# A hybrid attention/recurrence layer on one core: a front projection threaded through the transposes, and the sixth token block's closing products on GpSimd

## The chip, the core and the metric

One core of one Trainium2 chip runs the whole layer in one launch. The engines are TensorE (PE, with its weight loads PEld), VectorE (DVE), ScalarE (ACT), GpSimd (POOL) and SyncE (SP), which issues most DMAs. The metric is the device time of one execution in microseconds (us), as a median over several runs.

## The reference

The layer takes `x` of 1024 tokens by 1024 channels. It normalises the tokens, projects them with one wide matrix, runs two attention-like branches on the result, merges them, adds the residual, and ends in a squared-ReLU MLP and a last RMS norm. Cut to what the change touches:

```python
xn = rmsnorm(x, norm1_g[layer])
u = xn @ w_in[layer]                       # q, k, v of the attention come first
q_sb, k_sb, v_sb, ... = jnp.split(u, ...)
...
hn = rmsnorm(h, norm2_g[layer])
a = jnp.square(jax.nn.relu(hn @ w_ff1[layer]))
h = h + a @ w_ff2[layer]
return rmsnorm(h, final_g)
```

`rmsnorm(t, g)` is `t * rsqrt(mean(t*t) + 1e-6) * g` for each token.

## The kernel before

Everything is kept in float32 precision by splitting each operand of a matmul into a rounded part ("hi") and a remainder ("lo" = value minus hi). A product is then three matmuls: hi by hi, lo by hi, hi by lo. `hi_copy` (L156, on ACT) makes a hi part, `lo_sub` (L161, on DVE) makes a remainder. TensorE works through one long list of such triples, and the other engines prepare its operands and take its results out of the eight PSUM banks.

The tokens lie in eight blocks of 128 (`x` tile number `tb`). **The front** (the last part of the file, from `first_norms` on) does this for blocks 0 and 1, then for 2 and 3, then for 4 to 7: sum of squares on ACT and DVE, root on GpSimd (`inv_root`, L274), scaling on DVE (L664), and `norm_transpose`, in which TensorE turns the scaled tokens channel group by channel group (`kt` 0 to 7, tiles `xnt`, L131), ACT writes the hi part `xnh` with the gain (L348), and DVE the remainder `xnl` (L351). A bank of `xnt` is free again when its `xnl` is made. With one bank for the first projection and two for the values, five are left for `xnt`.

Between these steps `st.advance(n, 1)` takes n steps of the first job (`first_job`): the projection of the first head's queries and keys (`pjqk`, weights `wqk0`) and the projection to values (`pjv`, weights `wv`). The value weights come in four pieces of 1024 columns, each for two `kt`: raw `wvr`, hi `wvh`, remainder `wvl`. The body's steps are: four of `pjqk` for blocks 0 and 1, four "quarters" of `pjv` for blocks 0 and 1 (hi products of `kt` 0, 1; of `kt` 2, 3; remainder products of `kt` 0, 1; of `kt` 2, 3), four of `pjqk` for blocks 2 and 3, then the rest of `pjv`.

What sets the order: each engine runs its instructions in the order of its own list. That list follows the order in which the code is written, refined by a scheduler that honours priorities; `in_turn` and `after` add edges that fix the order on ACT and DVE while `turns["on"]` is true. A remainder that is "owed" (`owed_wlo`) is emitted later, by `lo_now()`; piece 1 of `wv` is such a one.

**The end** is `mlp_down`, whose last step treats the four column blocks of the last product m6 one after another. When block `tb` of four is done, DVE adds it to the residual tile `hb` of token block 2*tb+1 (`land`), ACT sums the squares of the right half (`half_ssq`), GpSimd adds that to the left half's (L2147) and takes the root (L274), and `finish_tokens` (L2156) makes the output. For an odd block the left half was multiplied with the gain earlier, so ACT only scales it (L2163); the right half takes `hb * root * gain` on DVE (L2166). The sixth token block (number 5, `NT - 3`) is finished while the last block (number 7) is summed, its right half after `summed_up`. The last block is done in quarters of 256 columns.

Of the kernel before, what the change touches and what calls it, by code (L numbers as in the profile page):

```python
# [9 lines left out]
F32 = mybir.dt.float32  # L10
# [4 lines left out]
ALU = mybir.AluOpType  # L15
# [7 lines left out]
NT = T // P  # L23
# [16 lines left out]
def kernel(  # L40
# [100 lines left out]
    def lo_now(behind=None):  # L141
        while owed_wlo:
            after(owed_wlo.pop()(), behind)
# [128 lines left out]
    def inv_root(mean, name):  # L272
        y = small.tile([P, 1], F32, tag="rs_y1", name=f"{name}_y", bufs=4)
        nc.gpsimd.tensor_tensor(out=y, in0=mean, in1=expo[:, 0:1], op=ALU.pow)  # L274
        return y
# [12 lines left out]
    last_power = [None]  # L288
# [33 lines left out]
    def norm_transpose(acts, half, b0, n, between=None):  # L322
# [17 lines left out]
        for kt in range(KT):  # L340
# [18 lines left out]
            )  # L359

# [84 lines left out]
    class Unit:  # L445
# [28 lines left out]
        def split(self, upto=None):  # L474
            self.load(upto)
            self.hl = self.hl or []
            for i, r in list(enumerate(self.raw))[len(self.hl) : upto]:
# [7 lines left out]
                if self.name == "wf1" or self.name == "wv" and i == 1:  # L485
                    hi_copy(h, r)
                    owed_wlo.append(lambda h=h, l=l, r=r: lo_sub(l, r, h))
                    continue
# [235 lines left out]
    def first_job():  # L724
# [17 lines left out]

        def v_steps(tb, kts):
# [1391 lines left out]
    def half_ssq(tb, n):  # L2135
# [10 lines left out]
        else:  # L2146
            nc.gpsimd.tensor_scalar(  # L2147
                out=ssq, in0=ssq, scalar1=1.0 / D, scalar2=fin[tb, 0], op0=ALU.mult, op1=ALU.add
            )

    def finish_tokens(tb, earlier=None, sides=(0, 1)):
        if sides[0] == 0:
            roots[tb] = inv_root(fin[tb, 1], f"fr{tb}"), slot(f"y{tb}")
        r, y = roots[tb]
        parts = 2 if tb == NT - 1 else 1
        for n, cs in (  # L2156
# [5 lines left out]
            if tb % 2 == 1 and n == 0:  # L2162
                after(nc.scalar.mul(y[:, cs], hres[tb][:, cs], r), earlier)  # L2163
# [93 lines left out]
    def mlp_down():  # L2257
        for i, (gi, c) in enumerate(steps):
# [11 lines left out]
            else:  # L2270
                for tb in range(3):
# [10 lines left out]
                for part in (slice(0, 256), slice(256, 512)):  # L2282
# [3 lines left out]
                    if part.start == 0:  # L2286
# [3 lines left out]
                        finish_tokens(NT - 3, squared, (0,))  # L2290
# [3 lines left out]
                summed_up = add(mean, mean, ssq)  # L2294
                finish_tokens(NT - 3, summed_up, (1,))
# [213 lines left out]
```

## Time and profile before

| | us |
|---|---|
| median of 3 runs | 1420.7 (1420.46 to 1420.71) |
| the profiled execution | 1420.47 |
| its span in the profile | 1418.7 |
| TensorE busy in it | 1408.6 (99%) |
| VectorE busy | 1088.1 (77%) |
| ScalarE busy | 684.6 (48%) |
| GpSimd busy | 143.3 (10%) |

The times of the views below are microseconds from the start of the span. A timeline row reads: start, duration, engine, line, operation, output from inputs, shape, how many were merged into the row, and in brackets how long the engine was idle before and what ended that. Several instructions of a row overlap a little, so a row of n with a single one beside it gives the distance between two starts. The span leaves out 1.8 us of the execution's time, before its first and after its last instruction.

### The profile page before, as it was taken

Reading aid. Unit: us, or ns where it says so; the run is one execution under the profiler, and the core shown is the slowest. Engines: PE = TensorE matmul, PEld = TensorE weight load, DVE = VectorE, ACT = ScalarE, POOL = GpSimd, SP = SyncE. Lnnn points to the kernel's source line nnn. Section 1 sums busy time; section 2 is a strip of 40 time slices with the busy share of each in tenths; the row PEclk is TensorE's granted clock in tenths of the full one; section 3 lists DMA queues with packets and bytes.
Section 4 is the critical chain, followed back from the end, with each engine's and each line's share of the span. In section 5 each row is a group of like instructions: output and inputs, shape, how many; then the busy total and the mean of one; then the engine's idle time right before and its main releaser. Section 6 shows DMA issues by size and latency. Waiting matters only on the chain.

```text
span 1418.7 us, 18796 instructions
## 1 busy us (share of the span) xinstructions
PE 1408.6 (99%) x6848; PEld 1184.0 (83%) x6848; DVE 1088.1 (77%) x1494; ACT 684.6 (48%) x1182; POOL 143.3 (10%) x339
## 2 busy tenths in 40 slices
PE   9999999999999999999999999999999999999998
PEld 8888888888888888888888888888888888888886
DVE  7579988988567888887788897677766657768766
ACT  6356676664243554433334764445444443434343
POOL 3012223210011031000000300000000000000031
PEclk9999999999999999999999999999999999999999
DMA  7124445545135685364585514444446974776725
GB/s 238 30 67 127 105 100 98 106 76 155 62 74 167 227 222 182 124 215 156 160 299 193 185 53 170 163 162 139 143 144 239 351 268 152 278 273 240 277 93 187
DMA packets 163173, 237.72 MB, mean 168 GB/s; under 512 B 26332, under 2 KB 93448, under 8 KB 163080
## 3 DMA queue, kind: packets, MB, share of 16 engines
q1 hardware_dynamic: 146056, 190.37, 40.0%
q0 software_dynamic: 11584, 34.61, 10.0%
q10 hardware_dynamic: 5440, 11.54, 2.3%
q8 instruction: 54, 0.88, 0.3%
q14 instruction: 39, 0.32, 0.1%
HBM read 168.32 MB, written 66.06 MB: 165 GB/s over the span
## 4 chain that ended last, share of the span: by engine, by line
PE 98%; DVE 1%; ACT 1%; DMA 0%; issue 0%; POOL 0%; SPq 0%; POOLq 0%; DVEq 0%; ACTq 0%
PE pm L128 21%; PE pX L128 9%; PE pW L128 6%; PE pY L128 6%; PE pjqk L128 6%; PE pga L128 4%; PE gX L128 4%; PE gY L128 4%; PE pjf L128 3%; PE pjq L128 3%; PE pys L128 3%; PE pji L128 3%; PE pyh L128 3%; PE pjv L128 3%; PE po L128 3%; PE z L128 2%
## 5 line engine op out<-in xcount | busy, mean ns | idle before, releaser
L156 ACT CAST whid<-w 128x1024 fp32r<-128x1024 f32 x30 | 31.6, 1054 | 154.4 <-PE pm L128 89.7
L826 DVE TENSOR_TENSOR_SCAN rm<-rm,bits 128x511 f32<-128x511 f32 (+7 forms) x72 | 87.3, 1220 | 17.0 <-ACT rm L804 16.9
L128 PE MATMUL pm<-whid,sh 128*128 128x512 f32 x240 | 93.4, 389 | 0.0
L128 PE MATMUL pm<-wlod,sh 128*128 128x512 f32 x240 | 93.4, 389 | 0.0
L128 PE MATMUL pm<-whid,sl 128*128 128x512 f32 x240 | 93.4, 389 | 0.0
L128 PE MATMUL pm<-tl,sh 128*128 128x512 f32 (+1 forms) x210 | 81.3, 387 | 0.0
L128 PE MATMUL pm<-th,sl 128*128 128x512 f32 (+1 forms) x210 | 81.3, 387 | 0.0
L128 PE MATMUL pm<-th,sh 128*128 128x512 f32 (+1 forms) x210 | 81.3, 387 | 0.0
L161 DVE TENSOR_TENSOR wlod<-w,whid 128x1024 fp32r<-128x1024 f32 x30 | 36.7, 1223 | 54.5 <-ACT whid L156 54.5
L161 DVE TENSOR_TENSOR sl<-sa,sh 128x1024 fp32r<-128x1024 f32 x56 | 68.2, 1218 | 0.3 <-ACT sh L156 0.3
L156 ACT CAST wTh<-pw 128x512 fp32r<-128x512 f32 (+2 forms) x96 | 43.8, 485 | 41.9 <-PE pw L131 41.0
L156 ACT CAST sh<-sa 128x1024 fp32r<-128x1024 f32 x56 | 57.2, 1046 | 7.8 <-DMA sa<-ad 7.8
L2143 POOL TENSOR_SCALAR fss<-fss 128x1 f32<-128x1 f32 x8 | 3.9, 482 | 562.0 <-ACT fsc L2138 561.5
L161 DVE TENSOR_TENSOR wTl<-pw,wTh 128x512 fp32r<-128x512 f32 (+2 forms) x96 | 49.9, 546 | 3.9 <-ACT wTh L156 3.7
L128 PEld LDWEIGHTS pm<-wlod,sh 128*128 128x128 f32 x240 | 45.0, 188 | 9.5
L128 PEld LDWEIGHTS pm<-whid,sl 128*128 128x128 f32 x240 | 45.1, 188 | 9.3
L128 PEld LDWEIGHTS pm<-whid,sh 128*128 128x128 f32 x240 | 45.1, 188 | 9.3
L169 DVE TENSOR_TENSOR bt<-bt,rm 128x511 f32<-128x511 f32 (+7 forms) x72 | 48.9, 685 | 3.5
L804 ACT ACTIVATE rm<-z 128x511 f32<-128x511 f32 (+4 forms) x96 | 48.0, 500 | 5.5 <-PE z L128 2.9
L128 PE MATMUL pX<-sqh,t1l 128*128 128x512 f32 x128 | 49.9, 390 | 0.0
L128 PE MATMUL pX<-sql,t1h 128*128 128x512 f32 x128 | 49.9, 390 | 0.0
L128 PE MATMUL pX<-sqh,t1h 128*128 128x512 f32 x128 | 49.8, 389 | 0.0
(930 smaller groups left out, 4432.4 us busy)
## 6 DMA issues: line engine op xcount, KB each, us to landing
w<-in_w_ff_dram SPq DMA_DIRECT2D x72, 512.0 KB, 4.7
sa<-ad SPq DMA_DIRECT2D x52, 512.0 KB, 6.4
ad<-a SPq DMA_DIRECT2D x32, 256.0 KB, 4.5
ad<-s SPq DMA_DIRECT2D x16, 512.0 KB, 3.3
tw<-in_w_out_dram POOLq DMA_DIRECT2D x24, 256.0 KB, 4.5
pr<-pd SPq DMA_DIRECT2D x10, 512.0 KB, 6.0
x<-in_x_dram SPq DMA_DIRECT2D x8, 512.0 KB, 7.8
xnl<-xnh POOLq DMA_DIRECT2D x8, 512.0 KB, 6.4
```

The lines of the kernel that those rows point to most:

```text
L128: return pe(nc.tensor.matmul(*a, **k))
L156: hi_last[0] = after(in_turn("act", nc.scalar.copy(dst, src)), hi_behind[0])
L161: nc.vector.tensor_tensor(out=dst, in0=src, in1=hi.bitcast(F32), op=ALU.subtract),
L169: return nc.vector.tensor_tensor(out=out, in0=a, in1=b, op=ALU.mult)
L804: nc.scalar.activation(rm[:, s0 + c0 - 1 : s0 + m - 1], z[:, c0:m], AF.Sigmoid, scale=-0.125)
L826: sc = nc.vector.tensor_tensor_scan(out=rr, data0=rr, data1=bits[:, 1024 - nk + a : 1024 - nk + b][:, ::-1], initial=rm[:, b : b + 1] if i ...
L2143: nc.gpsimd.tensor_scalar(out=ssq, in0=ssq, scalar1=1.0 / D, scalar2=EPS, op0=ALU.mult, op1=ALU.add)
```

## The change

Four edits in the front:

- `u_v.split()` now stands ahead of `norm_transpose(xn, 0, 2, 2)` instead of behind it, so the hi parts of the pieces 2 and 3 of `wv` are cast by ACT before the hi parts `xnh` of blocks 2 and 3.
- The remainder of piece 2 is made on GpSimd (L493). The remainders of the pieces 1 and 3 are both owed, and `lo_now()` stands behind `norm_transpose`; it pays them in the order in which they were owed.
- The last quarter of `pjv` (remainder products of `kt` 2, 3) moves behind the four `pjqk` steps of blocks 2 and 3.
- `norm_transpose` gets a callback `then`, called behind each `kt`; for blocks 2 and 3 it takes one `pjqk` step behind `kt` 4, 6 and 7. The number of steps taken up to the norms of blocks 4 to 7 is the same.

And two at the end:

- For block 5, GpSimd multiplies `hb` with the gain for the right half, in two quarters of 256 columns (`times_gain`, L2168): the first one once block 5's tile has landed, the second behind block 5's root.
- `finish_tokens(NT - 3)` then takes both halves on ACT behind the squares of the last block's first quarter: the right half is scaled from the product `y` instead of being made by DVE.

```diff
     def lo_now(behind=None):
         while owed_wlo:
-            after(owed_wlo.pop()(), behind)
+            after(owed_wlo.pop(0)(), behind)
...
-    def norm_transpose(acts, half, b0, n, between=None):
+    def norm_transpose(acts, half, b0, n, between=None, then=None):
...
+            if then:
+                then(kt)
...
-                if self.name == "wf1" or self.name == "wv" and i == 1:
+                if self.name == "wf1" or self.name == "wv" and i in (1, 3):
                     hi_copy(h, r)
                     owed_wlo.append(lambda h=h, l=l, r=r: lo_sub(l, r, h))
+                    continue
+                if self.name == "wv" and i == 2:
+                    hi_copy(h, r)
+                    ins = nc.gpsimd.tensor_tensor(
+                        out=l, in0=r, in1=h.bitcast(F32), op=ALU.subtract
+                    )
+                    after(ins, turns["dve"])
                     continue
...
         def body():
             ps = bank(f"{name}_0")
             yield from qk_steps(ps, 0, 0, 2)
-            for hi in (True, False):
-                for k0 in (0, 2):
-                    for tb in range(2):
-                        for kt in (k0, k0 + 1):
-                            v_part(tb, kt, hi, not hi)
-                    yield
+            for hi, k0 in ((True, 0), (True, 2), (False, 0)):
+                v_quarter(hi, k0)
+                yield
             yield from qk_steps(ps, 0, 2, 2)
+            v_quarter(False, 2)
+            yield
             ep(ps, 0)
...
+    def times_gain(tb, c0, behind):
+        cs = slice(c0, c0 + 256)
+        return after(
+            nc.gpsimd.tensor_tensor(
+                out=roots[tb][1][:, cs], in0=hres[tb][:, cs], in1=gfb[0][:, cs], op=ALU.mult
+            ),
+            behind,
+        )
...
-            if tb % 2 == 1 and n == 0:
-                after(nc.scalar.mul(y[:, cs], hres[tb][:, cs], r), earlier)
+            if tb % 2 == 1 and n == 0 or tb == NT - 3:
+                after(nc.scalar.mul(y[:, cs], (hres[tb], y)[n][:, cs], r), earlier)
...
                     landed = land(6, tb)
-                    half_ssq(2 * tb + 1, 1)
+                    if tb == 2:
+                        y = slot(f"y{NT - 3}")
+                        roots[NT - 3] = None, y
+                        product = times_gain(NT - 3, 512, None)
+                    half_ssq(2 * tb + 1, 1, product if tb == 2 else None)
                     if tb:
                         finish_tokens(2 * tb - 1, landed)
+                roots[NT - 3] = inv_root(fin[NT - 3, 1], f"fr{NT - 3}"), y
+                times_gain(NT - 3, 768, last_root[0])
...
-                        finish_tokens(NT - 3, squared, (0,))
+                        finish_tokens(NT - 3, squared)
...
-                summed_up = add(mean, mean, ssq)
-                finish_tokens(NT - 3, summed_up, (1,))
+                add(mean, mean, ssq)
                 finish_tokens(NT - 1)
...
     norm1((2, 3), half_means((2, 3)))
+    u_v.split()
+    st.advance(3, 1)
+    norm_transpose(xn, 0, 2, 2, then=lambda kt: st.advance(1, 1) if kt in (4, 6, 7) else None)
     lo_now()
-    st.advance(3, 1)
-    norm_transpose(xn, 0, 2, 2)
-    u_v.split()
-    st.advance(5, 1)
+    st.advance(2, 1)
```

How the lists of the engines move. First TensorE in the front, from the fifth pair of transposes of blocks 2 and 3 on (`x_165` and `x_169` are these blocks, `xnt_2` the banks they are turned into, `wvl_295` the remainder of `wv`'s piece 1). Before:

```order
L131 MATMUL xnt_2_358<-ident,x_169 128x128
L131 MATMUL xnt_2_363<-ident,x_165 128x128
L131 MATMUL xnt_2_363<-ident,x_169 128x128
L131 MATMUL xnt_2_368<-ident,x_165 128x128
L131 MATMUL xnt_2_368<-ident,x_169 128x128
L128 MATMUL pjv_316<-wvl_295,xnh_237 128x512
L131 MATMUL xnt_2_373<-ident,x_165 128x128
L131 MATMUL xnt_2_373<-ident,x_169 128x128
L128 MATMUL pjv_316<-wvl_295,xnh_237 128x512
L128 MATMUL pjv_321<-wvl_295,xnh_237 128x512 x2
L128 MATMUL pjqk_0_265<-xnh_229,wqk0whi 128x256
```

and now, from the same place on:

```order
L131 MATMUL xnt_2_364<-ident,x_169 128x128
L128 MATMUL pjqk_0_265<-xnh_229,wqk0whi 128x256
L128 MATMUL pjqk_0_265<-xnl_230,wqk0whi 128x256
L128 MATMUL pjqk_0_265<-xnh_229,wqk0wlo 128x256
L128 MATMUL pjqk_0_265<-xnh_229,wqk0whi 128x256
L131 MATMUL xnt_2_375<-ident,x_165 128x128
L128 MATMUL pjqk_0_265<-xnl_230,wqk0whi 128x256
L128 MATMUL pjqk_0_265<-xnh_229,wqk0wlo 128x256
L131 MATMUL xnt_2_375<-ident,x_169 128x128
L131 MATMUL xnt_2_380<-ident,x_165 128x128
L131 MATMUL xnt_2_380<-ident,x_169 128x128
```

The next rows of the list are the rest of `pjqk` with the last pair of transposes; it ends so:

```order
L128 MATMUL pjqk_0_265<-xnl_254,wqk0whi 128x256
L128 MATMUL pjqk_0_265<-xnh_253,wqk0wlo 128x256
L128 MATMUL pjqk_0_265<-xnh_253,wqk0whi 128x256
L128 MATMUL pjqk_0_265<-xnl_254,wqk0whi 128x256
L128 MATMUL pjqk_0_265<-xnh_253,wqk0wlo 128x256
L128 MATMUL pjv_322<-wvl_295,xnh_237 128x512 x2
L128 MATMUL pjv_327<-wvl_295,xnh_237 128x512 x2
L128 MATMUL pjv_322<-wvh_315,xnh_245 128x512
```

The four products with the remainder of piece 1 stood between the last transposes, and stand now behind all 24 products of `pjqk`, which are threaded among the last six transposes.

VectorE in the front, from the scaling of block 3 on. Before:

```order
L664 TENSOR_SCALAR x_169<-x_169,n_3_y 128x1024
L161 TENSOR_TENSOR wvl_295<-wvr_167,wvh_294 128x1024
L351 SCALAR_TENSOR_TENSOR xnl_230<-xnt_2_338,prm,xnh_229 128x256
L351 SCALAR_TENSOR_TENSOR xnl_230<-xnt_2_343,prm,xnh_229 128x256
L351 SCALAR_TENSOR_TENSOR xnl_238<-xnt_2_348,prm,xnh_237 128x256
L351 SCALAR_TENSOR_TENSOR xnl_238<-xnt_2_353,prm,xnh_237 128x256
L351 SCALAR_TENSOR_TENSOR xnl_246<-xnt_2_358,prm,xnh_245 128x256
L351 SCALAR_TENSOR_TENSOR xnl_246<-xnt_2_363,prm,xnh_245 128x256
L351 SCALAR_TENSOR_TENSOR xnl_254<-xnt_2_368,prm,xnh_253 128x256
L351 SCALAR_TENSOR_TENSOR xnl_254<-xnt_2_373,prm,xnh_253 128x256
L161 TENSOR_TENSOR wvl_379<-wvr_171,wvh_378 128x1024
L161 TENSOR_TENSOR wvl_383<-wvr_173,wvh_382 128x1024
```

and now:

```order
L673 TENSOR_SCALAR x_169<-x_169,n_3_y 128x1024
L351 SCALAR_TENSOR_TENSOR xnl_230<-xnt_2_344,prm,xnh_229 128x256
L351 SCALAR_TENSOR_TENSOR xnl_230<-xnt_2_349,prm,xnh_229 128x256
L351 SCALAR_TENSOR_TENSOR xnl_238<-xnt_2_354,prm,xnh_237 128x256
L351 SCALAR_TENSOR_TENSOR xnl_238<-xnt_2_359,prm,xnh_237 128x256
L351 SCALAR_TENSOR_TENSOR xnl_246<-xnt_2_364,prm,xnh_245 128x256
L351 SCALAR_TENSOR_TENSOR xnl_246<-xnt_2_375,prm,xnh_245 128x256
L351 SCALAR_TENSOR_TENSOR xnl_254<-xnt_2_380,prm,xnh_253 128x256
L351 SCALAR_TENSOR_TENSOR xnl_254<-xnt_2_391,prm,xnh_253 128x256
L161 TENSOR_TENSOR wvl_295<-wvr_167,wvh_294 128x1024
L161 TENSOR_TENSOR wvl_320<-wvr_173,wvh_319 128x1024
```

The remainder of piece 1 moves from ahead of the eight `xnl` to behind them, and that of piece 2 leaves VectorE.

GpSimd at the end, from block 3's sum on (`fss` are sums of squares, `fr_y` roots, `y_12322` the output tile of block 5). Now:

```order
L2160 TENSOR_SCALAR fss_1_12298<-fss_1_12298,fss_0_12054 128x1
L274 TENSOR_TENSOR fr_y<-fss_1_12298,expo 128x1
L2168 TENSOR_TENSOR y_12322<-hb_10470,gf 128x256
L2160 TENSOR_SCALAR fss_1_12324<-fss_1_12324,fss_0_12114 128x1
L274 TENSOR_TENSOR fr_y<-fss_1_12324,expo 128x1
L2168 TENSOR_TENSOR y_12322<-hb_10470,gf 128x256
L274 TENSOR_TENSOR fr_y<-f_ms,expo 128x1
```

Before, the same list held the two sums and the three roots alone; the two products of 256 columns are new, one ahead of block 5's sum and one between its root and the last block's. VectorE's list at the end is the same but for the product of block 5's right half, which is gone; ScalarE's has one scaling of 512 columns more, and the scaling of block 3's left half now stands behind the squares of block 5 instead of ahead of them. Behind the front and ahead of the end, the lists of all engines read as before.

More of the change, by code (lines that the diff above doesn't have):

```diff
@@ L273, in inv_root @@
         y = small.tile([P, 1], F32, tag="rs_y1", name=f"{name}_y", bufs=4)
-        nc.gpsimd.tensor_tensor(out=y, in0=mean, in1=expo[:, 0:1], op=ALU.pow)
+        last_root[0] = nc.gpsimd.tensor_tensor(out=y, in0=mean, in1=expo[:, 0:1], op=ALU.pow)
         return y
@@ L286, in mean_square @@
         return out
-    last_power = [None]
+    last_power, last_root = [None], [None]
     last_evac = [None]
@@ L741, in v_part, with v_quarter @@
                 matmul(ps, sh, wl, start=False, stop=kt == KT - 1)
+        def v_quarter(hi, k0):
+            for tb in range(2):
+                for kt in (k0, k0 + 1):
+                    v_part(tb, kt, hi, not hi)
         def v_steps(tb, kts):
@@ L2133, with half_ssq @@
     roots = {}
-    def half_ssq(tb, n):
+    def half_ssq(tb, n, behind=None):
         ssq = small.tile([P, 1], F32, tag=f"fss{n}", name=f"fss{tb}_{n}", bufs=8)
@@ L2146, in half_ssq @@
         else:
-            nc.gpsimd.tensor_scalar(
+            ins = nc.gpsimd.tensor_scalar(
                 out=ssq, in0=ssq, scalar1=1.0 / D, scalar2=fin[tb, 0], op0=ALU.mult, op1=ALU.add
             )
+            after(ins, behind)
+    def times_gain(tb, c0, behind):
[6 more added lines that the diff above has]
+        )
     def finish_tokens(tb, earlier=None, sides=(0, 1)):
-        if sides[0] == 0:
+        if tb not in roots:
             roots[tb] = inv_root(fin[tb, 1], f"fr{tb}"), slot(f"y{tb}")
```

## The prediction

> **What bounds the kernel now.** I read the page first, then who waited for whom on TensorE, then the timeline of the two stretches that the change touches.
>
> ```profile
> span 1418.7 us, 18796 instructions
> PE 1408.6 (99%) x6848; PEld 1184.0 (83%) x6848; DVE 1088.1 (77%) x1494; ACT 684.6 (48%) x1182; POOL 143.3 (10%) x339
> PE warm L128 <- POOL ident masks.py:199: 2.2, 1, 2.2
> PE po L128 <- DVE wTl L161: 0.3, 1, 0.3
> PE pjqk L128 <- DVE xnl L351: 0.3, 1, 0.3
> PE xnt L131 <- DVE xnl L351: 0.2, 1, 0.2
> ```
>
> TensorE is busy 99% of the span, and its waits add up to 3.0 us, of which 2.2 are the start. So the time is TensorE's list from end to end, plus what stands around it. A delay of TensorE in the front is paid in full, since there is no later wait that could take it up; other engines' savings count only where TensorE waits for them, or behind its last matmul.
>
> The front, where blocks 2 and 3 are turned:
>
> ```profile
> 16.45 0.39 PE L128 MATMUL pjv<-wvh,xnh 128*128 128x512 f32 x1
> 16.68 0.39 PE L128 MATMUL pjv<-wvh,xnl 128*128 128x512 f32 x1
> 17.82 1.25 PE L131 MATMUL xnt<-ident,x 128*128 128x128 f32 x10
> 18.23 3.03 ACT L348 ACTIVATE xnh<-xnt,prm 128x256 fp32r<-128x256 f32 x8 [3.13 <-PE xnt L131]
> 18.23 0.47 ACT L348 ACTIVATE xnh<-xnt,prm 128x256 fp32r<-128x256 f32 x1 [3.13 <-PE xnt L131]
> 17.60 1.22 DVE L161 TENSOR_TENSOR wvl<-wvr,wvh 128x1024 fp32r<-128x1024 f32 x1
> 18.74 3.23 DVE L351 SCALAR_TENSOR_TENSOR xnl<-xnt,prm,xnh 128x256 fp32r<-128x256 f32 x8
> 18.74 0.48 DVE L351 SCALAR_TENSOR_TENSOR xnl<-xnt,prm,xnh 128x256 fp32r<-128x256 f32 x1
> 19.28 0.83 PE L131 MATMUL xnt<-ident,x 128*128 128x128 f32 x4 [0.21 <-DVE xnl L351]
> 23.85 0.28 PE L128 MATMUL pjqk<-xnh,wqk0wlo 128*128 128x256 f32 x1
> 23.97 0.40 PE L128 MATMUL pjv<-wvh,xnh 128*128 128x512 f32 x1
> ```
>
> Ten transposes fill the five free banks; then TensorE waits until the first `xnl` frees one. It goes on at 19.28, 0.06 us after that `xnl` ends (18.74 + 0.48 = 19.22). From the rows I take the distances between starts: a transpose 0.11 ((1.25 - 0.27) / 9, the last lasting some 0.27), a product of 256 columns 0.12 (23.85 to 23.97), of 512 columns 0.23 (16.45 to 16.68), an `xnl` 0.39 ((3.23 - 0.48) / 7). At 23.97 the first product with pieces 2 and 3 starts. From 17.82 to there the work is 16 transposes (1.74), 24 products of `pjqk` (2.88) and four with piece 1's remainder (0.91): 5.5 of 6.15 us. The waits in it are worth 0.6 us, and that is all that threading could win here.
>
> **The front's cost.** First, what opens the chain does not move. The first `xnh` ends at 18.23 + 0.47 = 18.70, so the first `xnl` can start no earlier than about 18.75 even with VectorE free. Piece 1's remainder ended there anyway: taking it from ahead of the `xnl` wins at most 0.05 us.
>
> Behind them it costs. TensorE resumes at 19.28 and issues, up to the last pair of transposes, eleven products (1.32) and four transposes (0.44): the last pair starts at 21.04 and 21.15 and ends at 21.42, about 1 us later than now. ScalarE's last `xnh` starts at 21.45, where it now starts at 20.75 (18.23 + 3.03 less one of 0.5), ends at 21.95, and the last `xnl` lies at about 22.0 to 22.48 instead of ending at 21.97. Then comes piece 1's remainder with its 1.22, whose start overlaps the end before it by some 0.08: 22.40 to 23.62. TensorE, which has had nothing left since about 22.8, starts the four products with it at 23.68 and the first product of pieces 2 and 3 at 23.68 + 4 x 0.226 = 24.58. That is **0.6 us later** than 23.97. Were the last `xnl` not pushed at all, it would be 21.97 - 0.08 + 1.22 + 0.06 + 0.90 = 24.07, a loss of 0.1; one more slip of an `xnl` (0.39) makes it 1.0. The value is the worked chain, 0.6, and the ends 0.1 and 1.0.
>
> The other moved work has cover, if the loads are there. The casts of pieces 2 and 3 go into ScalarE's idle 3.13 us ahead of `xnh`:
>
> ```profile
> SPq L136 <- DMA wvr<-in_w_in_dram: 3.5, 4, 1.1
> 14.91 0.25 SPq L136 DMA_DIRECT2D prow<-in_lb_logits_dram  x1
> 16.27 0.25 SPq L136 DMA_DIRECT2D prow<-in_lb_logits_dram  x1
> 14.34 0.67 ACT L629 ACTIVATE n1scr<-x 128x512 f32<-128x512 f32 x1
> 21.10 2.05 ACT L156 CAST wvh<-wvr 128x1024 fp32r<-128x1024 f32 x2
> ```
>
> SyncE waits four times for a piece of `wvr`, and its issues at 14.91 and 16.27 follow the third and the fourth: so they land at about 14.87 and 16.23. ScalarE is free at 15.1 and casts them at 15.1 to 16.2 and 16.3 to 17.4, 0.8 us ahead of `xnh`. Without that cover a cast of 1.1 would delay `xnh` by what it overhangs.
>
> GpSimd's remainder of piece 2 waits for the first of these casts and stands behind block 3's root:
>
> ```profile
> 15.13 1.76 POOL L274 TENSOR_TENSOR n_y<-n_ms,expo 128x1 f32<-128x1 f32 x2 [7.39 <-DVE n_ms L1284]
> 16.93 0.75 DVE L664 TENSOR_SCALAR x<-x,n_y 128x1024 f32<-128x1024 f32 x1
> 24.73 0.55 POOL L269 TENSOR_TENSOR n_y<-n_ss,expo 128x1 f32<-128x1 f32 x1
> 25.32 0.75 DVE L664 TENSOR_SCALAR x<-x,n_y 128x1024 f32<-128x1024 f32 x1 [0.72 <-POOL n_y L269]
> 25.37 0.75 POOL L265 TENSOR_SCALAR n_ss<-n_ss 128x1 f32<-128x1 f32 x1
> masks.py:199 POOL TENSOR_SCALAR_AFFINE_SELECT ident<-ident 128x128 f32<-128x128 f32 x1 | 0.3, 287 | 0.0
> L862 POOL MEMSET wTh<- 128x128 f32 x32 | 10.7, 411 | 8.3 <-PE po L128 7.0 <-DVE bt L169 0.7 <-DMA od<-osb 0.5
> 1368.41 0.19 POOL L2143 TENSOR_SCALAR fss<-fss 128x1 f32<-128x1 f32 x1
> 34.88 3.65 PE L131 MATMUL xnt<-ident,x 128*128 128x128 f32 x32
> ```
>
> No row shows GpSimd on a wide product. From 128 columns in 0.287 us I take 2.24 ns a column: 0.57 us for 256 columns, 2.3 for 1024. The low end takes the 0.19 of a one-column sum as a fixed cost: (0.287 - 0.19) / 128 is 0.76 ns a column on top of it, 0.38 and 1.0; the high end is the 0.411 row's 3.2 ns: 0.82 and 3.3. GpSimd is free at 16.89. The rows at 25.3 show what follows: VectorE's scaling starts 0.04 after the root, GpSimd's next 0.05 later still, and that one lasts 0.75 instead of some 0.2 alone; it is held until the scaling is over. So the remainder runs from about 17.7 to 20.0 (21.0 at the high end). TensorE needs it at 25.0, and piece 3's remainder, on VectorE until 24.8, at 26.4: no cost. Roots of blocks 4 to 7 follow on GpSimd, with at most some 0.2 us lost behind VectorE's two remainders, and their tiles are wanted at 34.9. [...]
>
> **The end.** Behind the last matmul stands a chain of small steps:
>
> ```profile
> 1409.09 0.69 DVE L1284 TENSOR_TENSOR hb<-hb,pm 128x512 f32<-128x512 f32 x1 [1.37 <-PE pm L128]
> 1409.70 0.75 DVE L2166 SCALAR_TENSOR_TENSOR y<-hb,fr_y,gf 128x512 f32<-128x512 f32 x1
> 1410.64 0.27 POOL L2147 TENSOR_SCALAR fss<-fss,fss 128x1 f32<-128x1 f32 x1 [1.82 <-ACT fsc L2138]
> 1410.99 0.55 POOL L274 TENSOR_TENSOR fr_y<-fss,expo 128x1 f32<-128x1 f32 x1
> 1412.34 0.48 DVE L281 CUSTOM_DVE_ANT_0 fsc<-hb,fss 128x256 f32<-128x256 f32 x1
> 1413.02 0.74 DVE L2166 SCALAR_TENSOR_TENSOR y<-hb,fr_y,gf 128x512 f32<-128x512 f32 x1
> 1413.18 0.99 POOL L274 TENSOR_TENSOR fr_y<-f_ms,expo 128x1 f32<-128x1 f32 x1 [1.64 <-DVE f_ms L1284]
> 1414.20 0.91 ACT L2163 ACTIVATE y<-hb,fr_y 128x256 f32<-128x256 f32 x2 [1.38 <-POOL fr_y L274]
> ```
>
> The last root takes 0.99 where block 5's takes 0.55, because VectorE's product for block 5 (1413.02) runs beside it. The change takes that product away: **0.44 us won**, if the root starts no later. But the two new products lie ahead of it in GpSimd's list. Block 5's tile lands at 1409.78; by then VectorE's product for block 3 has run since 1409.70, and it holds GpSimd to 1410.45 by the same rule as at 25.3. The first quarter then ends at 1411.07, the sum lies at 1411.15 to 1411.42, the root at 1411.50 to 1412.05, the second quarter at 1412.13 to 1412.70. VectorE wants its squares of the last quarter at 1412.34, in the middle of that. If GpSimd does not hold VectorE, the root starts at 1413.18 as now: -0.44. If the squares wait for the second quarter, they start at about 1412.75, 0.41 later, and nothing is left of the gain: -0.03. With 0.82 a quarter and VectorE held all through it loses 0.47. One row bears on it:
>
> ```profile
> L2166 DVE SCALAR_TENSOR_TENSOR y<-hb,fr_y,gf x13: 476/744/779, 1368.4 to 1414.6; 128x512 f32<-128x512 f32 x11, 128x256 f32<-128x256 f32 x2
> ```
>
> The longest of these products, 779 ns against 744, is the one that starts at 1368.4, with the sum at 1368.41 beside it, which was not held. So VectorE can be the one that gives way. I take 0.0, nearest to the case in which it waits, with -0.44 and +0.47 as ends. ScalarE's extra scaling of block 5 (0.7) ends by 1413.7, ahead of 1414.2; block 3's left half, scaled later, is written out beside the rest. If that cover went, the last scaling would start late by the overhang.
>
> [...]
>
> The sum is +0.6 + 0.0 on the profiled execution's 1420.47, which is 0.2 below the median; on the median of 1420.7 it is **1421.3 us**. By itself it lies between 1420.7 + 0.1 - 0.4 = 1420.4 and 1420.7 + 1.0 + 0.4 = 1422.1.
>
> **The rivals.** *Not slower:* the front loses only its floor of 0.1 and the end keeps its 0.44: 1420.4. For it speaks that short GpSimd quarters would end ahead of 1412.34 (0.38 each gives 1412.32); against it that the last pair of transposes stands behind eleven products. *Slower by more:* at 16.93 GpSimd's wide product takes the turn before block 3's scaling. The scaling, held for 2.3 us, would end at 20.1, TensorE, which turns block 3 from 17.9 on, would stand still for it, and all behind it moves by 2.4: 1421.3 + 2.4 = 1423.7 (1422.4 to 1424.7 by the ends of that price). It decides when GpSimd starts first; the start rows have VectorE ahead by 0.05, and only the row at 1368.41 shows GpSimd unhindered. *No effect:* TensorE's 0.6 us of waits might be refilled just as the threading means, with piece 1's remainder ready in time; VectorE's list, eight `xnl` and then 1.22 us, leaves no room for that, so it gets little.
>
> **How the numbers follow.** The forecast gets 0.64, the not-slower rival 0.2, the scaling held up 0.09, no effect 0.03 (1420.7), anything else 0.04. The predicted time is 1421.3, and the range 1420.2 to 1422.1 leaves out the held scaling and little more. A difference of 0.2%, 2.8 us, is about what a measurement of this kernel can tell from no change: the forecast, the first rival and no effect all lie within it. Slower by more comes from the held scaling where it costs above 2.2 (0.06) and from the rest (0.01), faster by more from the rest alone (0.02).
>
> **What would show it.** In the changed profile TensorE should wait some 0.9 us for `wvl` ahead of the four products of piece 1, the first product of piece 2 should start near 24.6, and the last `xnh` near 21.45. GpSimd's wide remainder should start near 17.7 and last 2.3; block 3's scaling should start at 16.93. At the end the last root should take 0.55, and VectorE's last squares start near 0.4 later behind the matmuls than now. A first product of piece 2 ahead of 24.0 would make the front wrong, squares on time the end; a TensorE wait anywhere between 30 and 1400 us would make the whole sum wrong.

## The result, and the profile after

| | before | after |
|---|---|---|
| median, us | 1420.82 (1420.33 to 1421.09, 22 runs) | 1422.84 (1421.17 to 1424.58, 22 runs) |
| ratio | | 1.0015, 95% interval 1.0009 to 1.0021 |
| the profiled execution, us | 1420.47 | 1421.17 |
| its span, us | 1418.7 | 1419.4 |

The changed kernel is 2.0 us (0.14%) slower, where 0.5 was forecast (1421.3 against this median of 1420.82), and the time lies outside the range. Its executions fall into groups: 19 of 22 lie between 1422.5 and 1423.1, one at 1421.17, two near 1424.5. The profiled execution is the single one at 1421.17. What happens in the rest is seen in a second profile, that of the first experiment, and its rows stand here beside the first's.

The changed kernel's own execution (1421.17), from the head of its page and its waits on TensorE (total, times, longest):

```profile
span 1419.4 us, 18801 instructions
PE 1409.2 (99%) x6848; PEld 1184.0 (83%) x6848; DVE 1086.1 (77%) x1492; ACT 685.3 (48%) x1183; POOL 151.6 (11%) x342
PE warm L128 <- POOL ident masks.py:199: 2.2, 1, 2.2
PE pjv L128 <- DVE wvl L161: 0.6, 1, 0.6
```

and its timeline in the front, engine by engine:

```profile
15.90 1.06 ACT L156 CAST wvh<-wvr 128x1024 fp32r<-128x1024 f32 x1 [0.37 <-DMA wvr<-in_w_in_dram]
15.19 1.75 POOL L274 TENSOR_TENSOR n_y<-n_ms,expo 128x1 f32<-128x1 f32 x2 [7.64 <-DVE n_ms L1297]
17.03 2.94 POOL L493 TENSOR_TENSOR wvl<-wvr,wvh 128x1024 fp32r<-128x1024 f32 x1
16.98 0.75 DVE L673 TENSOR_SCALAR x<-x,n_y 128x1024 f32<-128x1024 f32 x1
22.01 0.48 DVE L351 SCALAR_TENSOR_TENSOR xnl<-xnt,prm,xnh 128x256 fp32r<-128x256 f32 x1 [0.27 <-ACT xnh L348]
23.68 1.19 PE L128 MATMUL pjv<-wvl,xnh 128*128 128x512 f32 x4 [0.62 <-DVE wvl L161]
24.72 0.40 PE L128 MATMUL pjv<-wvh,xnh 128*128 128x512 f32 x1
```

This front runs as forecast. GpSimd's remainder of piece 2 starts 0.05 behind block 3's scaling and is held until that ends: it lasts 2.94, of which 2.24 lie behind the scaling's end at 17.73, and takes 2.36 behind the guard below. The last `xnl` starts at 22.01, TensorE stands still 0.62 us for piece 1's remainder, and the first product of piece 2 comes at 24.72, where it came at 23.97: 0.75 us lost. But the cast of piece 2 starts only at 15.90, because that piece landed late in this execution (the bracket names the DMA). Now the same views of an execution of 1422.98:

```profile
PE xnt L131 <- DVE x L673: 1.6, 1, 1.6
PE pjv L128 <- DVE wvl L161: 0.6, 1, 0.6
14.95 1.09 ACT L156 CAST wvh<-wvr 128x1024 fp32r<-128x1024 f32 x1
15.15 1.76 POOL L274 TENSOR_TENSOR n_y<-n_ms,expo 128x1 f32<-128x1 f32 x2 [7.39 <-DVE n_ms L1297]
16.57 2.53 POOL L493 TENSOR_TENSOR wvl<-wvr,wvh 128x1024 fp32r<-128x1024 f32 x1
16.12 3.53 DVE L673 TENSOR_SCALAR x<-x,n_y 128x1024 f32<-128x1024 f32 x2 [0.17 <-POOL n_y L274]
16.94 2.71 DVE L673 TENSOR_SCALAR x<-x,n_y 128x1024 f32<-128x1024 f32 x1
19.71 1.20 PE L131 MATMUL xnt<-ident,x 128*128 128x128 f32 x9 [1.59 <-DVE x L673]
26.62 0.40 PE L128 MATMUL pjv<-wvh,xnh 128*128 128x512 f32 x1
```

Here the cast is over at 14.95 + 1.09 = 16.04. GpSimd's product is recorded from 16.57, while its second root is still running (15.15 + 1.76 = 16.91), and block 3's scaling, which can only start behind that root, lasts 2.71 us instead of 0.75. TensorE waits 1.59 us for it, and the first product of piece 2 starts at 26.62, another 1.90 later. Matmul by matmul, TensorE stands 2.66 us behind the kernel before at 29 us and 2.60 behind at 1334 us: what the front loses is paid in full.

The end of the changed kernel (the execution of 1421.17):

```profile
1410.80 0.74 DVE L2189 SCALAR_TENSOR_TENSOR y<-hb,fr_y,gf 128x512 f32<-128x512 f32 x1
1410.96 1.19 POOL L2168 TENSOR_TENSOR y<-hb,gf 128x256 f32<-128x256 f32 x1 [1.04 <-DVE hb L1297]
1412.99 0.42 DVE L1297 TENSOR_TENSOR hb<-hb,pm 128x256 f32<-128x256 f32 x1 [0.22 <-PE pm L128]
1413.00 0.73 POOL L2168 TENSOR_TENSOR y<-hb,gf 128x256 f32<-128x256 f32 x1
1413.44 0.56 DVE L281 CUSTOM_DVE_ANT_0 fsc<-hb,fss 128x256 f32<-128x256 f32 x1
1414.36 0.55 POOL L274 TENSOR_TENSOR fr_y<-f_ms,expo 128x1 f32<-128x1 f32 x1 [0.63 <-DVE f_ms L1297]
1414.94 0.91 ACT L2186 ACTIVATE y<-hb,fr_y 128x256 f32<-128x256 f32 x2 [0.40 <-POOL fr_y L274]
```

The last addition ends at 1412.99 + 0.42 = 1413.41 and the last scaling starts 1.53 later. The last addition of the kernel before:

```profile
1411.88 0.42 DVE L1284 TENSOR_TENSOR hb<-hb,pm 128x256 f32<-128x256 f32 x1 [0.22 <-PE pm L128]
```

There, that distance was 1414.20 - (1411.88 + 0.42) = 1.90. The last root takes 0.55 instead of 0.99, the squares 0.56 instead of 0.48. So the end wins 0.37, and the front loses 0.75 in the rare execution and some 2.6 in the usual one.

### The profile page after: what moved, and what is told of

It is laid out like the page before. It is cut to its first block, busy times and chain, and to the rows that moved or that the text cites. A ratio compares the mean times of both kernels' runs of the same rounds, so it can differ in the third digit from the quotient of the medians.

```text
span 1419.4 us, 18801 instructions
## 1 busy us (share of the span) xinstructions
PE 1409.2 (99%) x6848; PEld 1184.0 (83%) x6848; DVE 1086.1 (77%) x1492; ACT 685.3 (48%) x1183; POOL 151.6 (11%) x342
## 4 chain that ended last, share of the span: by engine, by line
PE 97%; DMA 1%; SPq 0%; DVE 0%; ACT 0%; issue 0%; POOL 0%; POOLq 0%; DVEq 0%; ACTq 0%
PE pm L128 21%; PE pX L128 9%; PE pW L128 6%; PE pY L128 6%; PE pjqk L128 6%; PE pga L128 4%; PE gX L128 4%; PE gY L128 4%; PE pjf L128 3%; PE pjq L128 3%; PE pys L128 3%; PE pji L128 3%; PE pyh L128 3%; PE pjv L128 3%; PE po L128 3%; PE z L128 2%
```

## The experiments

Times are medians, with the kernel before timed on the same chip in the same stretch: 1420.81 us (31 runs) beside the first four kernels, 1420.90 (33 runs) beside the next four, and 1420.77 beside the last four, each of which ran once. Where kernels timed on different chips are compared, it is by their distance from their own before. The interval of a ratio is some 0.0009 wide to each side, 1.3 us; smaller differences are read from the traces.

**The changed kernel again** (no edit).

> The changed kernel once more, for a second profile: its profiled execution took 1421.2 us, the median of the others 1422.8. Theory A (in most executions GpSimd's product for piece 2 gets its turn ahead of the scaling of block 3 on VectorE): median 1422.8 again, and a profile of an execution near 1422.8 shows the scaling of block 3 lasting or starting some 2 us late, with GpSimd's product unhindered beside it. Theory B (pieces 2 and 3 of the value weights land later in most executions, and ScalarE, which casts them ahead of xnh, is held until they land): such a profile shows the second of these casts ending 1 us and more behind 18.3 us, and the first xnh behind it. Theory C (the end: VectorE's last squares or GpSimd's last root are held): such a profile shows the front as in the first one and over 1.5 us more behind the last matmul.

Measured: 1422.99 (1422.89 to 1423.17, 11 runs), ratio 1.0015 [1.0006, 1.0024]. Its profiled execution is the second one shown above. The scaling of block 3 is what is lengthened.

**The front alone**: the end is that of the kernel before. The diff, against the changed kernel, shows the calls alone; the edits inside the helpers go back with them.

```diff
-                    if tb == 2:
-                        y = slot(f"y{NT - 3}")
-                        roots[NT - 3] = None, y
-                        product = times_gain(NT - 3, 512, None)
-                    half_ssq(2 * tb + 1, 1, product if tb == 2 else None)
+                    half_ssq(2 * tb + 1, 1)
...
-                roots[NT - 3] = inv_root(fin[NT - 3, 1], f"fr{NT - 3}"), y
-                times_gain(NT - 3, 768, last_root[0])
...
-                        finish_tokens(NT - 3, squared)
+                        finish_tokens(NT - 3, squared, (0,))
...
-                add(mean, mean, ssq)
+                summed_up = add(mean, mean, ssq)
+                finish_tokens(NT - 3, summed_up, (1,))
```

> The four edits of the front alone, the end as before the change. A and B: the whole loss is here, 1422.8 to 1423.3 (the end won 0.4 in the changed kernel's profile). C: 1421.2 to 1421.6, the 0.7 us of the profiled front.

Measured: 1423.45 (1422.17 to 1425.12, 9 runs), ratio 1.0020 [1.0011, 1.0030], 2.64 above before. All of the loss is in the front. Three of the nine runs lie between 1424.8 and 1425.2; without them the median would be 0.1 lower.

**The end alone**: the front is that of the kernel before. The diff shows the calls alone; the other edits of the front go back with them.

```diff
-    norm1((2, 3), half_means((2, 3)))
-    u_v.split()
-    st.advance(3, 1)
-    norm_transpose(xn, 0, 2, 2, then=lambda kt: st.advance(1, 1) if kt in (4, 6, 7) else None)
-    lo_now()
-    st.advance(2, 1)
+    norm1((2, 3), half_means((2, 3)))
+    lo_now()
+    st.advance(3, 1)
+    norm_transpose(xn, 0, 2, 2)
+    u_v.split()
+    st.advance(5, 1)
```

> The edits of the end alone, the front as before the change. A and B: 1420.4, or 0.4 us below the kernel before, as the changed kernel's profile has the last scaling 1.53 us behind the last tile where it was 1.90. C: 1422 and more. The prediction's middle value was no change, 1420.8.

Measured: 1420.43 (1420.34 to 1420.57, 11 runs), ratio 0.9997 [0.9988, 1.0006]. The end wins 0.38, as the two traces above say (0.37), though a ratio of this size is not told from 1. With the front's 2.64 the two halves sum to 2.26; the whole has 2.18.

**Piece 2's remainder on VectorE**, owed like those of the pieces 1 and 3; no wide product on GpSimd in the front.

```diff
-                if self.name == "wf1" or self.name == "wv" and i in (1, 3):
+                if self.name == "wf1" or self.name == "wv" and i in (1, 2, 3):
...
-                if self.name == "wv" and i == 2:
-                    hi_copy(h, r)
-                    ins = nc.gpsimd.tensor_tensor(
-                        out=l, in0=r, in1=h.bitcast(F32), op=ALU.subtract
-                    )
-                    after(ins, turns["dve"])
-                    continue
```

> The changed kernel, but the remainder of piece 2 is made by VectorE behind that of piece 1 instead of by GpSimd; the early casts and the moved products stay. A: the excess goes and the worked loss of the front stays: 1421.2. B: no change against the changed kernel, 1422.8. C: 1422.8.

Measured: 1421.18 (1420.9 to 1421.35, 11 runs), ratio 1.0002 [0.9994, 1.0011]. Of the 2.18 us, 1.81 are gone with this one instruction, and no run lies near 1423. TensorE's timeline has what is left:

```profile
23.77 1.19 PE L128 MATMUL pjv<-wvl,xnh 128*128 128x512 f32 x4 [0.63 <-DVE wvl L161]
24.80 0.40 PE L128 MATMUL pjv<-wvh,xnh 128*128 128x512 f32 x1
```

The wait for piece 1's remainder and the 0.8 us behind 23.97 are as in the execution of 1421.17. The early casts on ScalarE stay where the change put them, so they are not the cause.

**The product stays on GpSimd, but behind the scaling.**

```diff
                 if self.name == "wv" and i == 2:
                     hi_copy(h, r)
+                    turned = small.tile([P, 1], F32, tag="turned", name="turned")
+                    first = nc.gpsimd.tensor_copy(turned, xt[3][:, 0:1])
                     ins = nc.gpsimd.tensor_tensor(
                         out=l, in0=r, in1=h.bitcast(F32), op=ALU.subtract
                     )
-                    after(ins, turns["dve"])
+                    after(ins, first)
```

> The changed kernel, in which GpSimd first copies one column of the scaled block 3 into a small tile; the product for piece 2's remainder stands behind that copy, so it stays on GpSimd but cannot start ahead of the scaling's end. If the 1.9 us come from the turn that GpSimd takes ahead of that scaling (A): the scaling lasts 0.75, the product runs from about 17.8 to 20.1, block 3 is turned from 17.9 on, and the time is that of the kernel with piece 2 on VectorE, 1421.2 (1420.9 to 1421.4), with no execution near 1423. If a wide product on GpSimd in itself costs the front (it slows the eight xnl that now run beside it, or delays the later roots) (B): 1422 to 1423.

Measured: 1421.63 (1421.35 to 1421.8, 11 runs), ratio 1.0005 [0.9996, 1.0014]. Nothing lies near 1423. The timeline of GpSimd, VectorE and TensorE:

```profile
17.70 0.18 POOL L494 COPY turned<-x 128x1 f32<-128x1 f32 x1 [0.85 <-DVE x L675]
17.85 2.36 POOL L495 TENSOR_TENSOR wvl<-wvr,wvh 128x1024 fp32r<-128x1024 f32 x1
16.05 1.58 DVE L675 TENSOR_SCALAR x<-x,n_y 128x1024 f32<-128x1024 f32 x2 [0.17 <-POOL n_y L274]
24.77 0.39 PE L128 MATMUL pjv<-wvh,xnh 128*128 128x512 f32 x1
```

Both scalings together last 1.58, and the first product of piece 2 starts at 24.77: in the front the expectation holds. The median lies 0.2 above the interval that I gave it. It is 0.73 above its own before, where the kernel with piece 2 on VectorE is 0.37 above its own: 0.36 more. Up to 60 us the two kernels' TensorE run level; between 100 and 570 us this one falls back by 0.4, in steps mostly below 0.03, with no wait named. Its busy time is longer too, 1409.7 against 1408.7 us for the same 6848 matmuls, but one execution of the front alone (the one of 1423.66) has 1409.7 as well. What causes that is open.

**Piece 3 in place of piece 2 on GpSimd**, with no guard.

```diff
-                if self.name == "wf1" or self.name == "wv" and i in (1, 3):
+                if self.name == "wf1" or self.name == "wv" and i in (1, 2):
...
-                if self.name == "wv" and i == 2:
+                if self.name == "wv" and i == 3:
```

> The changed kernel with the remainder of piece 3 on GpSimd in place of that of piece 2; the pieces 1 and 2 are made on VectorE behind the eight xnl. Nothing makes GpSimd wait but the cast. If the turn is decided by whether the cast's end comes ahead of VectorE's scaling of block 3 (A): piece 3's cast ends near 17.1 to 17.4, after that scaling has started at 16.94, so the scaling lasts 0.75, the product starts behind it, and the time is 1421.2 (1420.9 to 1421.5). If GpSimd wins the turn whatever the order in which the two come (B): the scaling is held again and the time is 1422.9 or more.

Measured: 1421.04 (1420.74 to 1421.34, 11 runs), ratio 1.0000 [0.9992, 1.0009]. ScalarE, GpSimd and VectorE:

```profile
16.29 1.05 ACT L156 CAST wvh<-wvr 128x1024 fp32r<-128x1024 f32 x1 [0.30 <-DMA wvr<-in_w_in_dram]
17.42 2.40 POOL L493 TENSOR_TENSOR wvl<-wvr,wvh 128x1024 fp32r<-128x1024 f32 x1 [0.61 <-ACT wvh L156]
16.02 1.58 DVE L673 TENSOR_SCALAR x<-x,n_y 128x1024 f32<-128x1024 f32 x2 [0.17 <-POOL n_y L274]
```

The same product, with its cast ending 1.3 us later (17.34), comes when block 3's scaling is already running (from 16.84) and does it no harm. The time is 0.14 above its before, no more than with piece 2 on VectorE (0.37). So here neither the wide product nor its place in GpSimd's list costs anything that shows; its turn did.

**Piece 1's remainder back ahead of the eight `xnl`**, no wide product on GpSimd; the threading, the early casts and the end of the change stay. The edit is that of piece 2 on VectorE and, besides:

```diff
     norm1((2, 3), half_means((2, 3)))
+    lo_now()
     u_v.split()
```

> No wide product on GpSimd in the front (the pieces 2 and 3 on VectorE behind the eight xnl), and the remainder of piece 1 back ahead of the eight xnl; the threading, the early casts and the end of the change stay. If the worked front loss of 0.75 is piece 1's remainder made too late for TensorE (A): the wait for it goes, the first product of piece 2 starts at about 23.75 instead of 24.72 (before 23.97), and with the end's gain of 0.38 the time is 1420.2 (1420.0 to 1420.5) where before has 1420.8. If the loss is the last pair of transposes standing behind eleven products (B): a wait of some 0.7 for the last xnl takes the place of the one for piece 1, and the time is 1420.9 to 1421.2.

Measured: 1420.24 (1419.75 to 1420.45, 11 runs), ratio 0.9996 [0.9987, 1.0004]. TensorE's waits and timeline:

```profile
PE po L128 <- DVE wTl L161: 0.3, 1, 0.3
PE pjqk L128 <- DVE xnl L351: 0.3, 1, 0.3
10.06 0.39 PE L128 MATMUL pjqk<-xnh,wqk0whi 128*128 128x256 f32 x1 [0.28 <-DVE xnl L351]
22.81 1.08 PE L128 MATMUL pjv<-wvl,xnh 128*128 128x512 f32 x4
23.73 0.39 PE L128 MATMUL pjv<-wvh,xnh 128*128 128x512 f32 x1
```

No wait for `wvl` is left, the four products follow `pjqk` at once, and the first product of piece 2 starts 0.99 us ahead of the changed kernel's 24.72 and 0.24 ahead of before's 23.97. Of that, 0.18 and 0.13 are not the edit's: block 3's scaling already starts earlier in this execution (16.80, against 16.98 and 16.93). The one wait for an `xnl` (0.3) lies at 10.06 us, on blocks 0 and 1; for the last `xnl` of blocks 2 and 3 no wait is left to see, so the late transposes cost nothing that shows. This is the best version found, 0.66 below before in the medians; its interval includes no difference.

**The end without the gain on block 5's right half**: front as before, and the product of that half with the gain is left out (ScalarE scales it by the root alone).

```diff
-                        product = times_gain(NT - 3, 512, None)
-                    half_ssq(2 * tb + 1, 1, product if tb == 2 else None)
+                    half_ssq(2 * tb + 1, 1)
...
-                times_gain(NT - 3, 768, last_root[0])
...
-                after(nc.scalar.mul(y[:, cs], (hres[tb], y)[n][:, cs], r), earlier)
+                after(nc.scalar.mul(y[:, cs], hres[tb][:, cs], r), earlier)
```

> The front of the kernel before; the end of the change without GpSimd's two quarters: block 5's right half is scaled by its root without the gain, so that product is left out. It prices the quarters against the end alone (1420.43). If GpSimd's second quarter lengthens VectorE's last squares by 0.08 and costs nothing else (A): 1420.35, with squares of 0.485. If VectorE gave way for the whole overlap of 0.28 or the quarters also delay the sums and roots (B): 1420.1 to 1420.2. If they are free (C): 1420.43. The last root takes 0.55 in all three.

Measured: 1420.52 (1420.1 to 1420.94, 11 runs), ratio 0.9997 [0.9988, 1.0006]: 0.38 below its before, the same as the end alone. The squares are back at their old length:

```profile
1412.83 0.48 DVE L281 CUSTOM_DVE_ANT_0 fsc<-hb,fss 128x256 f32<-128x256 f32 x1
```

The trace shows 0.08 for the quarters; the medians don't resolve it. In this trace the quarters cost 0.08 and not the 0.2 or more of the reading B.

**Four kernels once more, one execution each.** The kernel before:

> The kernel before, one more profiled execution. In the six changed kernels profiled first, TensorE loses 0.32 to 0.34 between its 6500th and its last matmul against the profiled execution of before (in one place 16 us ahead of the end). If that belongs to the change (A), this execution keeps before's offset, 0.0 there. If it comes and goes with the execution (B), it can be here too: a TensorE offset of about 0.0 up to 1334 us and then either 0.0 or 0.33, with no wait named.

Measured: 1420.73. TensorE runs level with the first execution, within 0.1 us, up to 1334 us, and from there to the last matmul it falls back by 0.32. It loses that 16 us ahead of the end:

```profile
1395.25 0.39 PE L128 MATMUL pm<-whid,sh 128*128 128x512 f32 x1
1395.63 0.50 PE L128 MATMUL pm<-wlod,sh 128*128 128x512 f32 x1
1395.97 0.39 PE L128 MATMUL pm<-whid,sl 128*128 128x512 f32 x1
```

The starts stand 0.38 and 0.34 apart instead of 0.23 each, with no wait named. So it is nothing of the change: it comes and goes, and the profiled execution of before was one without it, which fits its lying 0.35 under its median.

The front alone, twice, and the changed kernel once more:

> The front alone, a second execution. The held scaling gives 1422.9 to 1423.5 with a scaling of 2.7; an execution with late loads 1421.5 to 1422.2 with a scaling of 0.75; of the ones near 1424.9 (three of nine timed) no profile shows the cause yet. If GpSimd's product can hold a second instruction of VectorE there (A), an execution of 1424.9 shows block 2's scaling or the first xnl lengthened by some 1.6 besides; if it is something outside the front (B), the first product of piece 2 starts at 26.6 in it as in the others.

> The same kernel, a third execution, for the same question: 1422.9 to 1423.5 with block 3's scaling at 2.7 and block 2's at 0.75, or 1424.9 with either a second instruction of VectorE lengthened by some 1.6 (A) or the front as in the others (B).

> The changed kernel, a third execution: 1422.8 with a held scaling of 2.7 in 19 cases of 22; 1421.2 with a cast of piece 2 that ends later than 16.9 and a scaling of 0.75 in one; near 1424.5 in two. The theory of the turn (A) says that the cast's end and the scaling's length go together in every one of them, whichever comes.

Measured: 1423.66, 1422.03 and 1422.90. The second is another execution with late loads; ScalarE, GpSimd and VectorE in it:

```profile
16.65 1.06 ACT L156 CAST wvh<-wvr 128x1024 fp32r<-128x1024 f32 x1 [0.36 <-DMA wvr<-in_w_in_dram]
15.95 1.75 POOL L274 TENSOR_TENSOR n_y<-n_ms,expo 128x1 f32<-128x1 f32 x2 [8.30 <-DVE n_ms L1297]
17.78 2.94 POOL L493 TENSOR_TENSOR wvl<-wvr,wvh 128x1024 fp32r<-128x1024 f32 x1
16.91 1.58 DVE L673 TENSOR_SCALAR x<-x,n_y 128x1024 f32<-128x1024 f32 x2 [0.17 <-POOL n_y L274]
```

All profiled executions with piece 2 on GpSimd and no guard, read from the same rows of each (us):

| execution | cast of piece 2 ends | block 2's scaling ends | block 3's scaling starts | product recorded from, to | block 3's scaling lasts |
|---|---|---|---|---|---|
| change, 1421.17 | 16.96 | 16.91 | 16.98 | 17.03, 19.97 | 0.75 |
| change, 1422.98 | 16.05 | 16.87 | 16.94 | 16.57, 19.10 | 2.71 |
| change, 1422.90 | 16.00 | 16.82 | 16.89 | 16.51, 19.05 | 2.71 |
| front, 1423.45 | 16.04 | 16.87 | 16.94 | 16.56, 19.09 | 2.71 |
| front, 1423.66 | 16.26 | 17.09 | 17.16 | 16.79, 19.31 | 2.71 |
| front, 1422.03 | 17.71 | 17.67 | 17.74 | 17.78, 20.72 | 0.75 |

In all six, the scaling is held where the cast ends ahead of block 2's scaling's end, and not where it ends behind it. The expectation for piece 3 compares the cast's end with the start of block 3's scaling, and that is not quite the line: in the two executions with late loads the cast ends 0.02 and 0.03 us ahead of that start, and the scaling is not held. There the product is recorded 0.04 to 0.05 us behind that start, so what goes with the outcome is the order of the two starts, by a margin as small as this. With piece 3 the margin is clear: its cast ends 0.50 us behind the scaling's start.

Neither execution near 1424.5 of the changed kernel, nor one of the three near 1425 of the front alone, came under the profiler, so what adds the last 1.6 us in those stays open. All five have a granted clock of 0.998, where most others have 0.999; but so have some of the others, among them the fastest of all (1419.75), so that alone does not explain it.

## Why the prediction was wrong

**What bounds the kernel** held: TensorE takes a delay of the front through to the end (2.66 us at 29 us, 2.60 at 1334).

**The front's cost** was right and slightly small: forecast 0.6, measured 0.75. The chain is the forecast's link by link (last `xnl` 22.01, four products at 23.68). The missing 0.14 is in the four products: forecast at 0.90, they take 1.04 from 23.68 to 24.72 behind the wait, and 0.92 where there is none (22.81 to 23.73 with piece 1's remainder first). That kernel also shows the cause to be the one named, piece 1's remainder behind the `xnl`.

**The casts** were covered as forecast, also when they came a microsecond late.

**GpSimd's remainder of piece 2 is the step that failed.** It said that VectorE's scaling of block 3 starts ahead of it, that it is held until 17.7, and that it costs nothing. In the usual execution it is the other way round: the product goes first, and the scaling is held for 2.16 us. The product's length was right (2.3 forecast, 2.36 behind the guard).

The step asked which of the two starts first behind the root, and took the answer, VectorE by 0.05 us, from the rows at 25.3. The instruction of GpSimd in those rows is a sum of one column. The next rows of the same view show such a sum starting late although its operand has been there for 0.57 us, and the first rows, in which two roots follow each other, show a root that does not:

```profile
15.13 0.94 POOL L274 TENSOR_TENSOR n_y<-n_ms,expo 128x1 f32<-128x1 f32 x1 [7.39 <-DVE n_ms L1284]
16.04 0.85 POOL L274 TENSOR_TENSOR n_y<-n_ms,expo 128x1 f32<-128x1 f32 x1
16.11 0.75 DVE L664 TENSOR_SCALAR x<-x,n_y 128x1024 f32<-128x1024 f32 x1 [0.17 <-POOL n_y L274]
26.03 0.24 ACT L295 ACTIVATION_READ_ACCUMULATOR n1scr<-x 128x1 f32 x1
26.20 0.55 POOL L269 TENSOR_TENSOR n_y<-n_ss,expo 128x1 f32<-128x1 f32 x1
26.79 0.75 DVE L664 TENSOR_SCALAR x<-x,n_y 128x1024 f32<-128x1024 f32 x1 [0.72 <-POOL n_y L269]
26.84 0.75 POOL L265 TENSOR_SCALAR n_ss<-n_ss 128x1 f32<-128x1 f32 x1
```

These are rows of the kernel before. The sum at 26.84 has had its operand since 26.27 (26.03 + 0.24), and starts 0.09 behind the root ahead of it and 0.05 behind VectorE's scaling. The second root starts at 16.04, 0.03 ahead of the first one's end (16.07) and 0.07 ahead of the scaling that waits for that first root. So the same trace held both orders, and the prediction took the one of the other kind of instruction. Why a sum keeps this distance and a root or a product does not, no run shows.

In the usual execution the product's operands are there at 16.05. It is recorded from 16.57, which is 0.34 ahead of the end of the root before it, whose result it does not need and block 3's scaling does. What it does until the root's end can be worked out from the table: from the end of block 2's scaling to the product's end is 2.22 to 2.23 us in all four held executions (19.10 - 16.87), and from the end of block 3's scaling to its end is 2.24 and 2.23 in the two others (19.97 - 17.73). The product behind the guard takes 2.36, with only the `xnl` of VectorE beside it. So it stands ready, waits, and takes the 0.07 us between the two scalings, in which block 3's is still waiting for its root. The two ends of the comparison are measured; that wait itself is argued from them. The root before it ends 0.04 behind block 2's scaling in all four, so the rows don't tell whether the product waits for that scaling or for that root. With the cast late, or with a later piece, block 3's scaling starts first, and the forecast's order holds.

The rival "slower by more" had this mechanism, with a chance of 0.09 and a price of 2.4. The price was a little high: 1.81 between the medians with piece 2 on GpSimd and on VectorE, and 1.90 at TensorE. The product holds the scaling from 16.94 to 19.10, 2.16 us, and the scaling then needs 0.55 more. The hold itself is in the trace: the scaling takes 2.71 against 0.75. I weighed such a hold of VectorE at the end of the kernel, where it is worth 0.08, and for this product only as a rival.

**The end** was taken at 0.0 and won 0.38. The mis-sized term is the hold on the squares: up to 0.41 was set against the root's 0.44, and it measured 0.08. The forecast let the squares start behind the second quarter, with their whole length still to come. They start on time, 0.03 behind the last addition, while the second quarter (1413.00 to 1413.73) has 0.29 to go, and end at 1414.00, 0.27 behind it, where they take 0.48 without it. So from the quarter's end they need 0.21 less than alone. The held scaling in the front shows the same: 0.75 unheld, 0.55 from the product's end, 0.20 less. The row thus fits squares that are held to the quarter's end; it does not show VectorE running on beside it. The hold was cheap because the quarter reached only 0.29 into the squares, and they needed 0.21 less behind it. The other links came as worked out: the first quarter is held until VectorE's product ends at 1411.55 and then needs 0.60 (0.57 forecast), and the last root takes 0.55.

The terms as measured: +0.75 + 1.81 - 0.38 = 2.18, which is the 2.18 of the first experiment. The 1.81 is a difference of that experiment itself; what the sum confirms is that the trace's 0.75 less the end's 0.38 gives the 0.37 by which the kernel with piece 2 on VectorE lies above its before.

## What to carry to other kernels

When wide work is given to an engine that holds another one up, as GpSimd's product held VectorE's scaling for 2.16 us here, list for each instruction when its operands are ready, not only when the one ahead of it ends: in four of six executions a product that stood ready went ahead of the scaling, though this was due 0.07 us behind the one before it, and the scaling lasted 2.71 us instead of 0.75. Read who starts first from rows of the same kind of instruction, and take merged rows apart for it. Give such work operands that come late, or tie it behind the instruction that must not wait; moving from the second piece to the third was worth 2.0 us here (0.14 above before instead of 2.18). And one profiled execution may be the exception: compare its time with the median before its rows are trusted.

## What the runs showed of the hardware that was not expected

- GpSimd's product of 1024 columns ran beside VectorE's `xnl`, which read PSUM and one SBUF tile, without lengthening them. In the execution of 1421.17 the first four start while the product is on (until 19.97), and all eight take 474 to 484 ns; in that of 1422.98, in which it was over by 19.10, ahead of the first `xnl`, they take 473 to 484. The tile view of `xnl` (count, shortest, median and longest in ns) in the two:

```profile
L351 DVE SCALAR_TENSOR_TENSOR xnl<-xnt,prm,xnh x8: 474/476/484, 18.7 to 22.0; 128x256 fp32r<-128x256 f32 x8
```

```profile
L351 DVE SCALAR_TENSOR_TENSOR xnl<-xnt,prm,xnh x8: 473/474/484, 20.6 to 23.9; 128x256 fp32r<-128x256 f32 x8
```

- In these traces a held instruction shows as a longer one, and from the end of the hold it needs less than alone. GpSimd's quarter of 256 columns lasts 0.73 where it starts beside VectorE's last addition, and 0.60 from the moment it is let go (1411.55 to 1412.15); the product of 1024 columns 2.36 and 2.24; so about 0.12 us less each. On VectorE it is 0.20 less for the scaling and 0.21 for the squares.
- TensorE loses some 0.33 us in the last product, most of it (0.25 to 0.38) at one place near 1395 us, in 11 of the 14 profiled executions, of before, of the change and of its variants, with no wait named. A profile's own time can be off its median by that much with nothing changed in the kernel: that of the kernel before lies 0.35 under its own (1420.47 and 1420.82).
